# Hybrid decoder layer: the last squares and the token scale of h from GpSimd to VectorE, with the scale's product with ones placed behind a fixed block of matmuls

## Chip, cores and metric

The kernel runs on one core of a Trainium2 chip. The metric is the device time of one execution in microseconds (us). TensorE is called PE, VectorE DVE, ScalarE ACT, GpSimd POOL and SyncE SP, as in the profile.

## What is computed

One layer over 16 meta tokens and 512 tokens of width 2048, in fp32, batch 1. The part that matters here is the seam between the output projection and the feed-forward network:

```python
o = concatenate([_rmsnorm(o_attn, g_attn_out), _rmsnorm(o_conv, g_conv_out)], axis=-1)
h = h + o @ w_out

n2 = _rmsnorm(h, g_ffn)
h = h + (silu(n2 @ w_gate) * (n2 @ w_up)) @ w_down      # D_FF = 5632
```

`_rmsnorm` multiplies a token by `rsqrt(mean(h*h) + 1e-6)` over its 2048 features and by a gain. Before the seam stand an input projection, stick-breaking attention over 8 heads and a gated short convolution.

## The kernel before

Activations are kept transposed: 128 features on the partitions, 512 tokens along the free dimension. Every fp32 operand of a large product is split into a high part (a cast on ACT, line 195 for activations, 652 for weights) and a low part (a subtraction on DVE, lines 196 and 653); a product is three matmuls, high x high, high x low, low x high (lines 750 to 752, and 729 to 731 in the output projection).

**Output projection.** A loop over 16 output tiles of 128 features (`OUT_TILES`). Each tile's two sums are scaled by the scales of the two groups and added to x (`residual`, lines 880 to 884), the result `hj` is written out, its squares are added to `acc_h` (`square_sum`: the square on ACT, line 214, the add on POOL, line 215), and the tile is cut into blocks of 256 tokens, which are mixed (lines 890 to 896, `mixed_blocks`) and split into activations `f0` to `f6`. Two of those seven, `f4` and `f6`, are gathered in DRAM and read back by POOL's DMA queue (`load_f`, line 834). The last tile (`i == KT - 1`) does its residual on DVE at a high priority, then the squares, then the mixed blocks.

**Gate and up.** 44 pairs (`pair_product`), each a Strassen-like product of seven blocks (`block_product`) with 24 matmuls each, on sums of weight quarters. The weight quarters come by SP's DMA queue (line 624); their sums are made on DVE (`add_quads`, line 659; lines 669 and 696), and each load of the next pair goes out when its buffer is free (`load_next`). The first pair takes its blocks in the order of activations 5, 0, 1, 2, 3, 4, 6. DVE combines the blocks out of PSUM between them (lines 781, 785, 788): line 785 reads the bank of `x` between the block on activation 4 and the one on activation 6, which goes on in the same bank.

**The scale of h.** The gain is applied ahead of the products, the token's scale behind them: `r_h`, that is `acc_h` after `h_scale`, multiplies the results of gate and up (lines 959 and 961). `h_scale` is called in the first pair behind the fourth block product (`fourth`). It calls `token_scale`: split `acc_h`, sum it over partitions by two matmuls with ones (lines 511 and 512, tile `ss_h`), add eps on DVE (line 513), then `rsqrt`: Ln and Exp on ACT (lines 202 and 203) and a Newton step of four instructions (lines 204 to 207). For h the low part of the split and the Newton step run on POOL (`eng=gp`), behind the last DMA issue of `load_f(6, 8)` (`tc.issue_after`). The scales of the attention and conv groups run the same function on DVE.

**Order.** A scheduler orders each engine's instructions by priority, data and its own estimates; `tc.high_priority` raises a block's priority, and `tc.keep_in_program_order` fixes an instruction's place on its engine as the program has it. Each engine executes its queue in that order.

## Time and profile before

| | |
|---|---|
| median of 3 runs | 2063.99 us (2063.92 to 2065.08) |
| profiled execution | 2063.16 us, span 2061.5 us |
| granted TensorE clock, mean | 0.999 |
| PE busy | 2048.7 us, 99% of the span |
| DVE busy | 1624.0 us, 79% |
| ACT busy | 1018.5 us, 49% |
| POOL busy | 369.7 us, 18% |

Busy time of PE is the union of pipelined matmuls, so that 99% still holds short waits. A row of the timeline gives start, duration, engine, line, operation, tiles (out<-in) and, in brackets, the idle time of the engine before it and what ended it. Times in the timeline count from the span's start. Buffer numbers are left out of tile names, so `x` is the bank of any pair.

### The profile page before, as it was taken

What the parts mean: (1) busy time and instruction counts of PE and PEld (TensorE: products, weight loads), DVE (VectorE), ACT (ScalarE), POOL (GpSimd) and SP (SyncE); (2) the same over time, 40 slices, a digit from 0 to 9 for tenths busy, and PEclk for the clock granted to TensorE, in tenths of its full rate; (3) what the DMA queues carried; (4) which work ended last, traced back from release to release, by engine and by line L of the source; (5) the groups of instructions that cost most, each with busy time, mean ns of one, the idle gap of its engine ahead of it and who ended that gap; (6) DMA issues with size and microseconds to landing.
All of it is one profiled execution on the core that took longest, in us unless ns stands there. A gap on an engine that the chain in (4) does not pass through costs nothing.

```text
span 2061.5 us, 39375 instructions
## 1 busy us (share of the span) xinstructions
PE 2048.7 (99%) x16086; PEld 1977.6 (96%) x16086; DVE 1624.0 (79%) x2140; ACT 1018.5 (49%) x1529; POOL 369.7 (18%) x490
## 2 busy tenths in 40 slices
PE   9999999999999999999999999999999999999999
PEld 8899999999998888999999999999999999999999
DVE  7877767533336678999898898898888988888888
ACT  7666566322224434555555555555555544444443
POOL 0111111010103445111111011011011243121111
PEclk9999999999999999999999999999999999999999
DMA  5122222222225555546555555465555899798764
GB/s 198 62 82 72 83 72 82 89 93 95 100 104 165 171 166 187 169 135 194 164 146 171 155 164 165 145 181 152 149 175 159 258 333 348 191 302 206 217 149 94
DMA packets 141669, 326.74 MB, mean 159 GB/s; under 512 B 12256, under 2 KB 60128, under 8 KB 141488
## 3 DMA queue, kind: packets, MB, share of 16 engines
q1 hardware_dynamic: 67456, 212.50, 31.9%
q0 software_dynamic: 74032, 111.73, 21.0%
q8 instruction: 126, 2.06, 0.4%
q14 instruction: 55, 0.45, 0.1%
HBM read 258.91 MB, written 65.27 MB: 157 GB/s over the span
## 4 chain that ended last, share of the span: by engine, by line
PE 95%; DVE 2%; DMA 1%; POOL 1%; issue 1%; ACT 1%; DVEq 0%; POOLq 0%; ACTq 0%
PE x L752 11%; PE x L750 11%; PE x L751 11%; PE z L752 5%; PE z L750 5%; PE z L751 5%; PE y L751 3%; PE y L750 3%; PE y L752 3%; PE po L731 3%; PE po L729 3%; PE po L730 3%; PE pv L182 2%; PE pv L184 2%; PE pv L183 2%; PE pu L184 1%
## 5 line engine op out<-in xcount | busy, mean ns | idle before, releaser
L652 ACT CAST sw_split<-sw_in 128x1024 fp32r<-128x1024 f32 (+1 forms) x534 | 527.3, 989 | 535.5 <-PE z L751 164.7
L653 DVE TENSOR_TENSOR sw_split<-sw_in,sw_split 128x1024 fp32r<-128x1024 f32 (+1 forms) x534 | 612.5, 1147 | 98.3 <-ACT sw_split L652 95.3
L752 PE MATMUL x<-f,sw_split 128*128 128x256 f32 x1408 | 388.1, 276 | 2.8 <-DVE sw_split L653 2.8
L750 PE MATMUL x<-f,sw_split 128*128 128x256 f32 x1408 | 388.1, 276 | 0.5 <-DVE u L785 0.3
L751 PE MATMUL x<-f,sw_split 128*128 128x256 f32 x1408 | 387.9, 276 | 0.2 <-DVE f L196 0.2
L752 PEld LDWEIGHTS x<-f,sw_split 128*128 128x128 f32 x1408 | 264.9, 188 | 3.2 <-DVE sw_split L653 3.1
L750 PEld LDWEIGHTS x<-f,sw_split 128*128 128x128 f32 x1408 | 265.0, 188 | 1.0 <-DVE u L785 0.5
L751 PEld LDWEIGHTS x<-f,sw_split 128*128 128x128 f32 x1408 | 264.9, 188 | 0.4 <-DVE f L196 0.4
L149 DVE TENSOR_TENSOR wlo<-raw,whi 128x512 fp32r<-128x512 f32 (+1 forms) x198 | 139.3, 707 | 127.5 <-ACT whi L148 126.9
L950 POOL DMA_DIRECT2D fd<-s x147 | 103.9, 908 | 686.7 <-DVE s L196 685.8
L148 ACT CAST whi<-raw 128x512 fp32r<-128x512 f32 (+1 forms) x198 | 121.4, 615 | 180.1 <-PE pu L183 64.0
L750 PE MATMUL z<-f,sw_split 128*128 128x256 f32 x704 | 193.6, 275 | 0.0
L751 PE MATMUL z<-f,sw_split 128*128 128x256 f32 x704 | 193.6, 275 | 0.0
L752 PE MATMUL z<-f,sw_split 128*128 128x256 f32 x704 | 193.6, 275 | 0.0
L659 DVE TENSOR_TENSOR sw_in<-sw_in 128x1024 f32<-128x1024 f32 (+1 forms) x144 | 164.6, 1143 | 6.9 <-DMA sw_in<-w_down 1.6
L752 PE MATMUL x<-ring,sw_split 128*128 128x256 f32 x608 | 167.3, 275 | 0.5 <-DVE sw_split L653 0.5
L750 PE MATMUL x<-ring,sw_split 128*128 128x256 f32 x608 | 167.2, 275 | 0.0
L751 PE MATMUL x<-ring,sw_split 128*128 128x256 f32 x608 | 167.2, 275 | 0.0
L750 PEld LDWEIGHTS z<-f,sw_split 128*128 128x128 f32 x704 | 132.2, 188 | 0.0
L752 PEld LDWEIGHTS z<-f,sw_split 128*128 128x128 f32 x704 | 132.2, 188 | 0.0
L751 PEld LDWEIGHTS z<-f,sw_split 128*128 128x128 f32 x704 | 132.2, 188 | 0.0
L752 PEld LDWEIGHTS x<-ring,sw_split 128*128 128x128 f32 x608 | 114.1, 188 | 0.7 <-DVE sw_split L653 0.7
(346 smaller groups left out, 5605.8 us busy)
## 6 DMA issues: line engine op xcount, KB each, us to landing
sw_in<-w_gu SPq DMA_DIRECT2D x176, 512.0 KB, 3.8
raw<-w_in SPq DMA_DIRECT2D x92, 512.0 KB, 3.3
fd<-s POOLq DMA_DIRECT2D x147, 256.0 KB, 5.3
sw_in<-w_down SPq DMA_DIRECT2D x96, 384.0 KB, 4.1
ring<-fd POOLq DMA_DIRECT2D x42, 768.0 KB, 16.9
sw_in<-w_out SPq DMA_DIRECT2D x30, 512.0 KB, 3.9
out_T<-d POOLq DMA_DIRECT2D x54, 256.0 KB, 4.6
sw_in<-w_down SPq DMA_DIRECT2D x16, 512.0 KB, 7.9
```

The costliest lines, as they stand in the source:

```text
L148: sc.copy(hi, raw)
L149: ve.tensor_tensor(lo, raw, hi.bitcast(F32), ALU.subtract)
L184: pe.matmul(ps, wl, ah[:, a:b], start=False, stop=k + i == last)
L652: sc.copy(hi, src)
L653: ve.tensor_tensor(lo, src, hi.bitcast(F32), ALU.subtract)
L659: return ve.tensor_tensor(sums[name], a, b, ALU.add)
L729: pe.matmul(ps, hi[:, kk], ah, start=k == 0, stop=False)
L730: pe.matmul(ps, hi[:, kk], al, start=False, stop=False)
L750: pe.matmul(p, hi[:, kk], act[:, 0, k], start=start and j == k == 0, stop=False, skip_group_check=skip)
L751: pe.matmul(p, hi[:, kk], act[:, 1, k], start=False, stop=False, skip_group_check=skip)
L752: pe.matmul(p, lo[:, kk], act[:, 0, k], start=False, stop=k == n - 1, skip_group_check=skip)
L950: gp.dma_start(fd[c][s][:, :, k], t[:, :, i])
```

## The change

The add of the last tile's squares goes to DVE and is written behind the mixed blocks. The token scale of h goes to DVE. Its first matmul with ones is kept in program order, which is behind the first pair's fourth block product. The order behind the last DMA issue of `load_f` is dropped.

```diff
-    def square_sum(acc, src, first, s=None):
+    def square_sum(acc, src, first, s=None, eng=gp):
...
-            gp.tensor_tensor(acc, acc, s, ALU.add)
+            eng.tensor_tensor(acc, acc, s, ALU.add)
...
-    def token_scale(acc, dst, count, name, work, eng=ve):
+    def token_scale(acc, dst, count, name, work, eng=ve, in_order=False):
...
-        pe.matmul(ps, ones_r, sh, start=True, stop=False)
+        first_sum = pe.matmul(ps, ones_r, sh, start=True, stop=False)
+        if in_order:
+            tc.keep_in_program_order(first_sum)
...
             with tc.high_priority(1 << 20):
                 residual(ve)
-                square_sum(acc_h, hj, False, wide_tmp("h", bufs=2))
                 mixed_blocks()
+                square_sum(acc_h, hj, False, wide_tmp("h", bufs=2), ve)
...
-        with tc.high_priority(1 << 20), tc.issue_after(last_f.ins):
-            token_scale(acc_h, acc_h, D, "h", (w[:, 0], w[:, 1], a[:, 0], a[:, 1], b), gp)
+        with tc.high_priority(1 << 20):
+            token_scale(acc_h, acc_h, D, "h", (w[:, 0], w[:, 1], a[:, 0], a[:, 1], b), ve, True)
```

`load_f` no longer returns its last issue. In the built program the same instructions stand on every engine but for six that pass from POOL to DVE. Their order differs only around the seam: on PE the two matmuls with ones stand directly behind the first pair's fourth block product and ahead of the block on activation 4, where before 14 and 16 matmuls of that block stood ahead of them; 13 instead of 5 matmuls of the second pair's first block stand ahead of the first pair's last block. In the next pair the same boundary moves by 6 matmuls. On DVE the order of some 70 instructions changes, and SP's three loads behind the last tile's write go out in another order.

More of the change, by code (lines that the diff above doesn't have):

```diff
@@ L833, in load_f @@
         for part in range(2):
-            last = gp.dma_start(acts[s][:, part, :n], fx[s][:, part, :n], max_dma_last_dim=4096)
-        return last
+            gp.dma_start(acts[s][:, part, :n], fx[s][:, part, :n], max_dma_last_dim=4096)
     after(3, scale_c)
@@ L916, in hybrid_layer @@
                 with tc.high_priority(1 << 20):
-                    last_f = load_f(6, 8)
+                    load_f(6, 8)
         if i < KT - 1:
```

## The prediction

> **What bounds the kernel now.** I read the page first: the share of each engine, then the chain that ended last.

> ```profile
> PE 2048.7 (99%) x16086; PEld 1977.6 (96%) x16086; DVE 1624.0 (79%) x2140; ACT 1018.5 (49%) x1529; POOL 369.7 (18%) x490
> PE 95%; DVE 2%; DMA 1%; POOL 1%; issue 1%; ACT 1%; DVEq 0%; POOLq 0%; ACTq 0%
> ```

> TensorE (PE) sets the time, so a change is worth the TensorE time that it gives back. The view of waits, for PE alone, tells where such time lies.

> ```profile
> PE x L752 <- DVE sw_split L653: 3.3, 3, 2.3
> ...
> PE ss_h L512 <- POOL work_r L196: 1.2, 1, 1.2
> ```

> Both rows belong to the seam between the output projection and the first gate/up pair, where the scale of h is made. The timeline of PE there:

> ```profile
> 797.12 0.28 PE L750 MATMUL z<-f,sw_split 128*128 128x256 f32 x1
> ...
> 799.89 0.28 PE L750 MATMUL x<-f,sw_split 128*128 128x256 f32 x1
> ...
> 802.61 0.28 PE L750 MATMUL z<-f,sw_split 128*128 128x256 f32 x1
> ...
> 805.33 0.28 PE L750 MATMUL x<-f,sw_split 128*128 128x256 f32 x1
> ...
> 807.09 0.50 PE L511 MATMUL ss_h<-work_r,ones_r 128*128 128x512 f32 x1
> 807.42 0.28 PE L752 MATMUL x<-f,sw_split 128*128 128x256 f32 x1
> 807.54 0.28 PE L750 MATMUL x<-f,sw_split 128*128 128x256 f32 x1
> 809.05 0.50 PE L512 MATMUL ss_h<-work_r,ones_r 128*128 128x512 f32 x1 [1.23 <-POOL work_r L196]
> ...
> 812.07 0.38 PE L750 MATMUL x<-f,sw_split 128*128 128x256 f32 x1 [0.32 <-DVE u L785]
> ...
> 819.93 0.28 PE L751 MATMUL x<-f,sw_split 128*128 128x256 f32 x1
> 822.54 0.58 PE L752 MATMUL x<-f,sw_split 128*128 128x256 f32 x1 [2.34 <-DVE sw_split L653]
> ...
> 825.48 0.33 PE L750 MATMUL x<-f,sw_split 128*128 128x256 f32 x1
> ...
> 826.60 0.28 PE L750 MATMUL z<-f,sw_split 128*128 128x256 f32 x1
> ```

> A block of 24 products takes 2.72 us undisturbed (799.89 to 802.61), a product 0.113. From 797.12 to 826.60, 29.48 us, PE did eight blocks (8 x 2.72 = 21.8) and the two products with ones (0.23 each by their spacing): 22.2 us of work, so **7.3 us were lost**. That is the most that the change can bring, but for the wait of the first products on the last tile (near 796), which it leaves alone. Of it 2.5 us is the hole from 820.0 to 822.54, and 1.4 the slow products behind it: 13 steps from 822.54 to 825.48 took 2.94 us, where 13 x 0.113 = 1.5 would do. The view by windows shows that clock:

> ```profile
> 822.50:825.60 3.10, 3.06 (x14) 3.06 (x15) 3.10 (x4) 2.42 (x3) 0.00 (x0) 0.50 0.11 18
> ```

> (columns: window, length, busy PE, PEld, DVE, ACT, POOL, granted clock, DMA share, GB/s.) The clock was halved after the hole.

> **What is removed.** GpSimd's timeline has the six moved instructions (L215, L196, L204 to L207); three of them, and the L215 of the tile before:

> ```profile
> 786.17 1.28 POOL L215 TENSOR_TENSOR acc_h<-acc_h,sw_in 128x512 f32<-128x512 f32 x1 [0.46 <-ACT sw_in L214]
> ...
> 796.03 9.21 POOL L215 TENSOR_TENSOR acc_h<-acc_h,w 128x512 f32<-128x512 f32 x1 [2.41 <-ACT w L214]
> 807.11 1.89 POOL L196 TENSOR_TENSOR work_r<-acc_h,work_r 128x512 fp32r<-128x512 f32 x1 [1.87 <-ACT work_r L195]
> ...
> 815.53 2.16 POOL L205 TENSOR_TENSOR work_b<-work_b,work_a 128x512 f32<-128x512 f32 x1
> ```

> The add of the last squares took 9.21 us against 1.28 one tile earlier, while VectorE was full. It delays the two products; PE then waits 1.23 for the low part, and the hole at 820 comes from the last four instructions, which VectorE waits for with its weight splits queued behind (row 820.66 below). All of that goes. GpSimd has only DMA issues left, and these wait for VectorE's data; the order behind the reload's last issue, which the edit also drops, had no other use.

> **What is added.** VectorE (DVE), timeline:

> ```profile
> 792.17 0.68 DVE L881 TENSOR_TENSOR w<-w,sw_in 128x512 f32<-128x512 f32 x1
> 792.76 1.22 DVE L653 TENSOR_TENSOR sw_split<-sw_in,sw_split 128x1024 fp32r<-128x1024 f32 x1
> 793.90 0.69 DVE L883 TENSOR_TENSOR w<-w,sw_in 128x512 f32<-128x512 f32 x1
> ...
> 796.31 0.42 DVE L196 TENSOR_TENSOR f<-src,f 128x256 fp32r<-128x256 f32 x1
> 796.64 1.22 DVE L659 TENSOR_TENSOR sw_in<-sw_in 128x1024 f32<-128x1024 f32 x1
> ...
> 805.52 1.23 DVE L659 TENSOR_TENSOR sw_in<-sw_in 128x1024 f32<-128x1024 f32 x1 [1.43 <-DMA sw_in<-w_gu]
> ...
> 807.79 1.49 DVE L196 TENSOR_TENSOR f<-src,f 128x256 fp32r<-128x256 f32 x1
> ...
> 816.45 2.32 DVE L659 TENSOR_TENSOR sw_in<-sw_in 128x1024 f32<-128x1024 f32 x1
> 820.66 0.69 DVE L959 TENSOR_TENSOR u<-u,acc_h 128x512 f32<-128x512 f32 x1 [1.89 <-POOL acc_h L207]
> ```

> In a full queue a 128x512 instruction takes 0.60 us of VectorE (792.17 to 792.76), a 128x1024 one 1.135 (792.76 to 793.90), a 128x256 one 0.335 (796.31 to 796.64). Five of the six cost 0.60; L206 ran on VectorE in the scale of the conv group:

> ```profile
> L206 DVE TENSOR_SCALAR sw_in<-sw_in x1: 427/427/427, 633.2 to 633.2; 128x512 f32<-128x512 f32 x1
> ```

> so 0.34 of queue. Together 3.3 us. Against that, VectorE's own instructions beside GpSimd's were stretched: 807.79 by 1.07 (1.49 against 0.42) and 816.45 by 1.10. Those 2.2 us come back.

> **Walk through the new order.** In the built program the new VectorE order from 796.64 on is: L215, L653, L196, L669, L893, L653, L196, L895, L659, L196, L196, L788, L653, L196 (the low part of acc_h), L653, L781, L513, L653, L659, L204, L785. The squares are there (ScalarE's L214 had released GpSimd at 796.0). The first twelve are four of 128x1024 (4.54), seven of 128x256 (2.35) and L215 (0.60): 796.64 + 7.5 = 804.1. The split L653 of the sixth weight needs its cast by ScalarE, which can start when L659 ends (803.2):

> ```profile
> 802.75 1.06 ACT L652 CAST sw_split<-sw_in 128x1024 fp32r<-128x1024 f32 x1 [0.55 <-PE x L751]
> ```

> so cast to 804.3, L653 from 804.35 to 805.5, and the low part of acc_h ends at 805.5 + 0.68 = 806.2. The two products with ones now stand ahead of the whole block that starts at 805.33. The first goes at once, as its cast of acc_h is done by 804.9; the second, due at 805.56, waits to 806.2, and every product of the first two pairs is queued behind it, where before 14 products of the next block ran ahead of the first and 16 ahead of the second: **0.65 lost**, and 0.1 at the first product after a wait (807.42 came 0.33 behind 807.09, not 0.23). Then L653 (806.1), L781 (807.2), L513 (807.55; its sums are there from 806.7, so it holds nothing up), L653 (808.15), L659 (809.3), L204 (810.4; Ln and Exp end near 809.6), L785 from 811.0 to 811.45. PE meanwhile runs the block to 806.45 + 2.72 = 809.2, then 13 products of the next pair's first block, which the program puts there, to 810.65; the seventh block of the pair needs L785: **0.8 + 0.1 lost**. The next pair's L785 stands behind L205 to L207 and the gate work that this delays; nothing in before shows its wait. Bounds: 0, and another 0.9; I take 0.45, halfway, as VectorE has no idle time left up to there in the walk. The 0.1 at the first product with ones included, the new order loses 0.75 + 0.9 + 0.45 + 0.1 = 2.2 us. **The sum: 7.3 - 2.2 = 5.1 us less.** L204 to L207 now end near 816, and the first scaling L959 waits for nothing; no hole near 820, so no halved clock.

> **The load that moves.** The add L659 of the first pair's third mixed weight goes behind L669, so the three weight loads that their buffers release go out in another order: the one that the next pair's L659 (809.3 in the walk) reads is last of three, not first, and issued at 803.6 instead of 797.89.

> ```profile
> 797.89 0.33 SPq L624 DMA_DIRECT2D sw_in<-w_gu  x1
> sw_in<-w_gu SPq DMA_DIRECT2D x176, 512.0 KB, 3.8
> f<-fx POOLq DMA_DIRECT2D x2, 1024.0 KB, 12.6
> GB/s 289 283 238 156 88 263 378 401 416 430 401 401 437 394 361 370 418 397 401 393 438 393 418 385 385 393 410 418 426 410 410 410 410 418 221 33 25 0 0 0
> ```

> (the last row: 790 to 810 us in 40 slices.) It took 7.6 us in before (797.89 to 805.5), under the reload of the activations; the median of all is 3.8. So it lands between 807.4 and 811.2, and costs 0 to 1.9 us. I take 0: the transfers run at some 400 GB/s to 807.3 and then stop, and the bytes are the same, so the last load lands near 808, over 1 us early.

> The profiled execution took 2063.16, 1.66 over its span, and becomes 2058.1; the median of the runs shown is 0.83 higher: **2058.9 us**. 0.2% is 4.1 us, about what a measurement of this kernel can tell from no change.

> **The rivals.** *Late load.* The moved load takes 7.6 us again: VectorE stops at L659, L785 follows, PE loses 1.9 more: 2060.8. For it speaks the same reload; against it, that the reload is nearly through by 803.6.

> *No halved clock in the timed runs.* A hole of 2.5 us halved the clock here, for about 3 us. If the hole lies otherwise to whatever measures it, before does not pay the 1.4, and the gain is 3.7: 2060.3. [...]

> *VectorE becomes the bound (slower).* In the pairs that follow VectorE is nearly full:

> ```profile
> 830.00:840.00 10.00, 10.00 (x91) 10.00 (x90) 9.07 (x12) 4.51 (x6) 0.00 (x0) 1.00 0.68 203
> 840.00:850.00 10.00, 10.00 (x91) 10.00 (x90) 9.90 (x12) 6.30 (x9) 0.95 (x2) 1.00 0.16 55
> ```

> If its backlog is not worked off, each of the 42 pairs behind the second loses 0.45 at its L785 too: 18.9 - 5.1 = 13.8 us more, 2077.8; slower than before from twelve such pairs on (5.1 / 0.45). Against it: a pair takes PE seven blocks, 19.0 us, and the busy shares of 91% and 99% overstate VectorE, since the 12 instructions of a row overlap by 0.09 each (85% without that); some 2.9 us a pair are free, so the backlog goes in a pair or two.

> *No effect.* PE's lost time returns at other waits, as L785 moved: within 1 us of 2064.

> **How the numbers follow.** Forecast 0.72 (nine tenths of it beyond 4.1 us), late load 0.08, no halved clock 0.12, no effect 0.04, VectorE the bound 0.04. Faster by over 0.2%: 0.65; within: 0.31; slower: 0.04. The range: at the low end only the wait for the low part of acc_h stays, 7.3 - 0.85 = 6.4 us less, 2057.6; at the high end late load and no halved clock together, 5.1 - 1.9 - 1.4 = 1.8 less, 2062.2.

> **What would show it.** Right: L215 on VectorE near 796.6 in some 0.68; L512 waiting about 0.65 for DVE, no longer POOL; a wait at L750 for L785 of 0.7 to 0.9; no wait over 2 us and no clock of 0.5 near 822; the 826.60 row some 5 us earlier. Wrong: a wait of L659 for its load near 810, a new hole over 1 us, waits for L785 in pair after pair, or the end unmoved though the seam is shorter.

## The result, and the profile after

| | before | after |
|---|---|---|
| median of the timed runs | 2064.74 us (8 runs, 2063.92 to 2065.85) | 2058.67 us (8 runs, 2058.21 to 2059.78) |
| profiled execution | 2063.16 us, span 2061.5 | 2058.70 us, span 2056.9 |

The ratio is 0.9972, with a 95% interval of 0.9963 to 0.9981: 5.8 us faster by the ratio, 6.1 by the medians, against 5.1 forecast from the seam. The two profiled executions differ by 4.5 us.

In the kernel after, line numbers behind 511 are two higher than before (512 is 514, 653 is 655, 659 is 661, 750 to 752 are 752 to 754, 785 is 787), and one higher behind `load_f` (959 is 960). So the rows named L752 here are the high x high products that were L750. The page's shares and the chain of the kernel after:

```profile
PE 2046.7 (100%) x16086; PEld 1976.0 (96%) x16086; DVE 1623.2 (79%) x2146; ACT 1016.0 (49%) x1529; POOL 351.5 (17%) x484
PE 96%; DVE 2%; ACT 1%; issue 1%; DMA 0%; POOL 0%; SPq 0%; DVEq 0%; ACTq 0%; POOLq 0%
```

GpSimd (POOL) has six instructions fewer and VectorE (DVE) six more; GpSimd, with 1% of the chain before, has 0% now. The view of waits for PE, cut to the seam:

```profile
PE x L752 <- DVE u L787: 1.5, 2, 1.3
PE ss_h L514 <- DVE work_r L196: 0.5, 1, 0.5
```

The 2.3 us wait for VectorE's weight split and the 1.2 us wait for GpSimd's subtraction are gone; three shorter ones, of 1.32, 0.49 and 0.21 us, stand in their place (the first row holds two). The timeline of PE there, with the products in front of each wait (start, duration):

```profile
805.22 0.40 PE L511 MATMUL ss_h<-work_r,ones_r 128*128 128x512 f32 x1
806.11 0.50 PE L514 MATMUL ss_h<-work_r,ones_r 128*128 128x512 f32 x1 [0.49 <-DVE work_r L196]
806.45 0.28 PE L752 MATMUL x<-f,sw_split 128*128 128x256 f32 x1
...
810.56 0.28 PE L752 MATMUL x<-f,sw_split 128*128 128x256 f32 x1
812.15 0.39 PE L752 MATMUL x<-f,sw_split 128*128 128x256 f32 x1 [1.32 <-DVE u L787]
...
830.43 0.28 PE L754 MATMUL x<-f,sw_split 128*128 128x256 f32 x1
830.91 0.38 PE L752 MATMUL x<-f,sw_split 128*128 128x256 f32 x1 [0.21 <-DVE u L787]
```

By spacing, with 0.23 us for a product with ones and 0.113 for another, the first wait costs 0.89 - 0.23 = 0.66 us, the product behind it 0.11 more, the second wait 1.59 - 0.11 = 1.48 and the third 0.48 - 0.11 = 0.37. The clock stays whole where it was halved before (windows, column PEclk):

```profile
822.50:825.60 3.10, 3.10 (x30) 3.10 (x29) 2.56 (x3) 1.65 (x3) 0.00 (x0) 1.00 0.09 12
```

VectorE's timeline shows why the second wait is longer than the forecast's 0.8:

```profile
796.54 0.68 DVE L215 TENSOR_TENSOR acc_h<-acc_h,w 128x512 f32<-128x512 f32 x1
...
805.37 0.68 DVE L196 TENSOR_TENSOR work_r<-acc_h,work_r 128x512 fp32r<-128x512 f32 x1
...
809.94 1.22 DVE L661 TENSOR_TENSOR sw_in<-sw_in 128x1024 f32<-128x1024 f32 x1 [0.69 <-DMA sw_in<-w_gu]
811.08 0.68 DVE L204 TENSOR_TENSOR work_b<-work_a 128x512 f32<-128x512 f32 x1
811.68 0.42 DVE L787 SCALAR_TENSOR_TENSOR u<-x,sides 128x256 f32<-128x256 f32 x1
...
821.50 0.68 DVE L960 TENSOR_TENSOR u<-u,acc_h 128x512 f32<-128x512 f32 x1
```

Up to the low part of `acc_h` (805.37) all is as walked. Then L661 waits 0.69 us for its weights, the load that the change moved, and L787, which PE waits for, is as much later. The first scaling, L960, waits for nothing any more.

To compare executions, take the starts of matmuls number 5000 and 5500 (counted from 0, in order of start), on either side of the seam; before, then after:

```profile
791.16 0.28 PE L751 MATMUL y<-f,sw_split 128*128 128x256 f32 x1
856.29 0.28 PE L751 MATMUL x<-f,sw_split 128*128 128x256 f32 x1
```

```profile
791.05 0.28 PE L753 MATMUL y<-f,sw_split 128*128 128x256 f32 x1
851.92 0.28 PE L753 MATMUL x<-f,sw_split 128*128 128x256 f32 x1
```

That is 65.1 us of seam before and 60.9 after. The stretch from matmul 5500 to the last took 1201.0 and 1200.9. All profiled executions of this study can be cut so (us; the last column is the whole profiled execution):

| kernel (label of its run) | start of no. 100 | 100 to 5000 | seam, 5000 to 5500 | 5500 to last | time |
|---|---|---|---|---|---|
| before | 20.20 | 770.95 | 65.14 | 1201.02 | 2063.16 |
| before_again | 20.12 | 771.05 | 66.03 | 1200.87 | 2063.93 |
| before_third | 21.19 | 771.04 | 64.78 | 1201.04 | 2063.90 |
| before_fourth | 20.91 | 771.05 | 65.13 | 1200.87 | 2063.81 |
| after | 20.08 | 770.97 | 60.87 | 1200.86 | 2058.70 |
| after_again | 20.10 | 771.02 | 60.40 | 1201.07 | 2058.74 |
| squares_only | 20.79 | 770.93 | 64.68 | 1200.87 | 2063.11 |
| scale_only | 20.16 | 771.05 | 62.26 | 1200.89 | 2060.62 |
| scale_only_again | 21.00 | 771.09 | 62.27 | 1201.16 | 2061.78 |
| newton_gp | 20.13 | 771.04 | 63.58 | 1201.23 | 2062.20 |
| newton_gp_again | 20.25 | 771.00 | 63.27 | 1201.02 | 2061.79 |
| free_sum | 19.66 | 771.05 | 60.83 | 1200.86 | 2058.32 |
| t3_before | 20.16 | 770.94 | 65.30 | 1200.86 | 2063.10 |
| l785_high | 20.21 | 771.02 | 60.25 | 1200.31 | 2057.84 |

Two columns vary: the seam, which the change is about, and the first 20 us, the program's first loads and products, which no kernel here touches and which ended anywhere from 19.66 to 21.19 us. The seam went from 65.3 (mean of four) to 60.6 (mean of two): **4.6 us** is what the profiles show of the change.

### The profile page after: what moved, and what is told of

The parts are those of the page before. It is cut to its first block, busy times and chain, and to the rows that moved or that the text cites. A ratio compares the mean times of both kernels' runs of the same rounds, so it can differ in the third digit from the quotient of the medians.

```text
span 2056.9 us, 39370 instructions
## 1 busy us (share of the span) xinstructions
PE 2046.7 (100%) x16086; PEld 1976.0 (96%) x16086; DVE 1623.2 (79%) x2146; ACT 1016.0 (49%) x1529; POOL 351.5 (17%) x484
## 3 DMA queue, kind: packets, MB, share of 16 engines
HBM read 258.91 MB, written 65.27 MB: 158 GB/s over the span
## 4 chain that ended last, share of the span: by engine, by line
PE 96%; DVE 2%; ACT 1%; issue 1%; DMA 0%; POOL 0%; SPq 0%; DVEq 0%; ACTq 0%; POOLq 0%
PE x L752 11%; PE x L754 11%; PE x L753 11%; PE z L752 6%; PE z L753 6%; PE z L754 6%; PE y L752 3%; PE y L753 3%; PE y L754 3%; PE po L732 3%; PE po L733 3%; PE po L731 3%; PE pv L182 2%; PE pv L184 2%; PE pv L183 2%; PE pu L184 1%
## 5 line engine op out<-in xcount | busy, mean ns | idle before, releaser
L752 PE MATMUL x<-f,sw_split 128*128 128x256 f32 x1408 | 387.6, 275 | 1.8 <-DVE u L787 1.5
L752 PEld LDWEIGHTS x<-f,sw_split 128*128 128x128 f32 x1408 | 264.3, 188 | 2.3 <-DVE u L787 1.9
L752 PE MATMUL z<-f,sw_split 128*128 128x256 f32 x704 | 193.6, 275 | 0.0
L661 DVE TENSOR_TENSOR sw_in<-sw_in 128x1024 f32<-128x1024 f32 (+1 forms) x144 | 163.4, 1134 | 5.5 <-DMA sw_in<-w_down 0.8
L752 PE MATMUL x<-ring,sw_split 128*128 128x256 f32 x608 | 167.2, 275 | 0.0
L752 PEld LDWEIGHTS z<-f,sw_split 128*128 128x128 f32 x704 | 132.2, 188 | 0.0
## 6 DMA issues: line engine op xcount, KB each, us to landing
sw_in<-w_gu SPq DMA_DIRECT2D x176, 512.0 KB, 3.7
raw<-w_in SPq DMA_DIRECT2D x92, 512.0 KB, 3.3
sw_in<-w_out SPq DMA_DIRECT2D x30, 512.0 KB, 4.0
sw_in<-w_down SPq DMA_DIRECT2D x16, 512.0 KB, 7.8
```

The costliest lines, as they stand in the source:

```text
L661: return ve.tensor_tensor(sums[name], a, b, ALU.add)
L752: pe.matmul(p, hi[:, kk], act[:, 0, k], start=start and j == k == 0, stop=False, skip_group_check=skip)
```

## The experiments

**The theory after the result:** the seam's losses came from GpSimd's part of the scale, above all from the Newton step; VectorE does the same six instructions in 3.3 us and gives back most of the time. Rivals: the 9.21 us add of the squares was the loss, or the scale's new place on PE was the gain, or the half clock was.

### The kernel before, again: before_again, before_third, before_fourth

No edit.

> The kernel before, unchanged, to see how its hole near 820 us and the halved clock behind it vary between executions. Theory (the halved clock depends on how the hole lies to a measuring stretch): the hole is again 2.3 to 2.6 us, but the granted clock behind it, or elsewhere near the seam, differs from the first profile, and the executions that are slower than the first profiled one (2063.16 us) lose the difference there; between 0 and 3 us at half clock. Rival (the spread of the runs lies elsewhere): the seam from 797 to 827 us takes 29.5 us again with the same 1.4 us at half clock, and a time above 2064 shows outside the seam.

It took 2063.93 us. The hole is there again, the half clock is not, and the add took another course. GpSimd, VectorE and PE near 796:

```profile
796.04 1.50 POOL L215 TENSOR_TENSOR acc_h<-acc_h,w 128x512 f32<-128x512 f32 x1 [2.41 <-ACT w L214]
808.19 1.82 POOL L196 TENSOR_TENSOR work_r<-acc_h,work_r 128x512 fp32r<-128x512 f32 x1 [10.66 <-ACT work_r L195]
```

```profile
796.33 1.49 DVE L196 TENSOR_TENSOR f<-src,f 128x256 fp32r<-128x256 f32 x1
```

```profile
797.87 0.39 PE L751 MATMUL x<-f,sw_split 128*128 128x256 f32 x1 [1.26 <-DVE f L196]
```

The add took 1.50 us instead of 9.21, VectorE's L196 beside it 1.49 instead of 0.42, and PE stood 1.07 us longer for it (1.64 between the two products' starts, 0.57 otherwise). So there are two outcomes, called the race for the add from here on: 9.21 us on GpSimd with 0.42 on VectorE, or 1.50 with 1.49. And with the add done at 797.5, GpSimd idled 10.66 us and began its subtraction no sooner: **the add by itself delayed nothing**, because ACT's cast of `acc_h` (L195, at 807.50 here) stands later in its queue.

> The kernel before, unedited, profiled a third time: its timed runs lie from 2062.4 to 2065.4 us, and two profiled executions showed different losses (2063.16 with 3.4 us at half clock behind the 2.6 us hole and GpSimd's add at 9.21 us; 2063.93 with no half clock, the add at 1.50 and PE standing 1.07 longer at 797). Theory: the add's outcome (0 or 1.1 us) and the half clock (0, or 1.4 to 1.7 for a stretch of 3.4 us, twice that for 6.8) vary from execution to execution, and the time follows: a third profile shows one of the four combinations, with the hole of 2.6 us in it every time; 2062 to 2066. Rival: the losses go with the program, and the profile repeats one of the two shown with a time that they don't explain.

> The kernel before, unedited, profiled a fourth time, as in the third: the hole of 2.6 us at the same product; the add at either about 9.2 or about 1.5 us, and in the second case 1.07 us more at the product at 797; a stretch at half clock or none; time 2062 to 2066, the higher the more of the two it has.

They took 2063.90 and 2063.81 us, with the add at 9.21 us in both, and the hole of 2.61 us between starts. The third had no half clock, the fourth had it; the windows behind the hole, third and then fourth:

```profile
823.50:826.70 3.20, 2.64 (x22) 2.45 (x22) 3.20 (x4) 2.71 (x3) 0.00 (x0) 1.00 0.22 42
```

```profile
823.50:826.70 3.20, 3.20 (x16) 3.20 (x16) 3.17 (x5) 2.95 (x4) 0.00 (x0) 0.50 0.23 51
```

PE was busy for all 3.20 us at half clock (16 products), and for 2.64 at full clock (22). What filled the rest is in PE's and ACT's timeline of the third:

```profile
827.16 0.39 PE L750 MATMUL z<-f,sw_split 128*128 128x256 f32 x1 [1.01 <-ACT sides L777]
```

```profile
823.97 1.28 ACT L962 ACT_TABLE_LOAD   x1 [4.33 <-DVE g L961]
825.27 0.64 ACT L962 ACTIVATE g<-g 128x512 f32<-128x512 f32 x1
825.81 1.03 ACT L652 CAST sw_split<-sw_in 128x1024 fp32r<-128x1024 f32 x1
826.74 0.36 ACT L777 COPY sides<-z 128x256 f32<-128x256 f32 x1
```

At full clock PE reaches the block on `z` earlier and there waits 1.01 us for ACT's copy, which stands behind the gate's table load and activation, which waited 4.33 us for VectorE's L961, which follows the Newton step. In PE's timeline the hundredth product behind the hole started 12.90 and 13.12 us after it in the two executions with half clock, 12.81 in both without: the half clock cost 0.1 to 0.3 us, not 1.4. Both losses have one cause, the late scale.

The mean granted clock on record for each timed run says the same: a stretch of 3.4 us at half clock lowers the mean over 2061 us to 0.999. Of the 49 runs of before in the two larger sets, 17 had 1.0 and took 2063.8 us in the mean; 32 had 0.999 or 0.998 and took 2064.2. All 16 timed runs of the kernel after had 1.0.

Of the theory on the spread, the parts varied as expected, but not the time with them: what moved it were the add's race (66.03 of seam against 65.0) and the first 20 us (up to 1.1).

### The squares alone on VectorE: squares_only

The edit is against the kernel before.

```diff
-                square_sum(acc_h, hj, False, wide_tmp("h", bufs=2))
                 mixed_blocks()
+                square_sum(acc_h, hj, False, wide_tmp("h", bufs=2), ve)
```

> The change's first part alone: the last tile's add of squares on VectorE behind the mixed blocks; the split's low part and the Newton step of the scale of h stay on GpSimd, the product with ones free. Theory (the time was lost to what GpSimd does behind the add: the low part and the Newton step, with VectorE's weight splits queued behind the first scaling): PE waits for the low part from GpSimd for over 1 us and again 2 to 3 us at a hole while the Newton step runs on GpSimd, so hardly anything is gained: 2063 to 2066 us. Rival (the 9.21 us add of squares was the whole cost, since all else waits for it): most of the gain is there, 2058.5 to 2060.

2063.02 us, a ratio of 0.9994 (0.9986 to 1.0003): no gain that can be measured. PE's timeline:

```profile
805.43 0.50 PE L511 MATMUL ss_h<-work_r,ones_r 128*128 128x512 f32 x1 [1.07 <-ACT work_r L195]
807.29 0.80 PE L514 MATMUL ss_h<-work_r,ones_r 128*128 128x512 f32 x1 [1.13 <-POOL work_r L196]
814.63 0.39 PE L754 MATMUL x<-f,sw_split 128*128 128x256 f32 x1 [1.05 <-DVE sw_split L655]
823.85 0.38 PE L752 MATMUL x<-f,sw_split 128*128 128x256 f32 x1 [0.96 <-ACT sides L777]
```

The first product with ones comes 1.7 us earlier, and the waits are split up but remain: GpSimd's subtraction, its Newton step behind VectorE's weight split, ACT's copy. The rival that the add was the loss falls. The clock was halved here too, from 806.8 to 810.2, and the seam of 64.68 has that in it.

### The scale alone on VectorE: scale_only, scale_only_again

The edit is against the kernel before.

```diff
-        with tc.high_priority(1 << 20), tc.issue_after(last_f.ins):
-            token_scale(acc_h, acc_h, D, "h", (w[:, 0], w[:, 1], a[:, 0], a[:, 1], b), gp)
+        with tc.high_priority(1 << 20):
+            token_scale(acc_h, acc_h, D, "h", (w[:, 0], w[:, 1], a[:, 0], a[:, 1], b), ve, True)
```

> The change's second part alone: split, Newton step and the placed product on VectorE as in the changed kernel; the last tile's add of squares stays on GpSimd ahead of the mixed blocks. Theory (the hole came from the Newton step on GpSimd, and the add of squares is late but can be borne): the add still takes some 9 us, the product's low part is waited for by 1 to 1.5 us, but no hole over 2 us and no halved clock: 2058 to 2060 us. Rival (the 9.21 us add was the whole cost): 2063 to 2065. Second rival (both parts are needed, each gives about half): 2061 to 2062.

2061.04 us, 0.9987 (0.9978 to 0.9996). The hole is gone; 3.0 us of the seam's 4.6 are there without the squares. What is missing is in PE's waits:

```profile
797.92 0.38 PE L753 MATMUL x<-f,sw_split 128*128 128x256 f32 x1 [1.26 <-DVE f L196]
811.76 0.50 PE L514 MATMUL ss_h<-work_r,ones_r 128*128 128x512 f32 x1 [2.01 <-DVE work_r L196]
```

The first is the race for the add again (1.50 us on GpSimd here). The second is the low part of `acc_h`: it is at 811.02 on VectorE, behind three more weight instructions and a wait of 1.40 us for a load, where the whole change has it at 805.37. So the squares on VectorE are worth 1.6 us with the scale there, most of it the race, and 0.6 without it (65.27 against 64.68).

> The scale alone on VectorE, with the square add left on GpSimd, profiled again. The first profile took 2060.6 us with the add at 1.50 us, 1.07 us more at 797 and a wait of 2.0 us at the second product with ones; its runs lie from 2059.3 to 2063.7. Theory: with the add at 9.2 us the stall at 797 is gone and the time is 2059.3 to 2059.6, unless the clock is halved behind the 2.0 us wait, which adds 1.7 or more. Rival: the add's outcome doesn't move the end and the time is 2060.6 with either.

2061.78 us, with the add at 1.50 us again, so the outcome at 9.2 was not seen and the question of its price in this kernel stays open. The clock was halved here, from about 800.2 to 803.6, yet the seam is the same to 0.01 us (62.27 against 62.26): the products came later to the second product with ones, and its wait shrank from 2.01 us to 0.3. The 1.16 us between the two executions lie at the start (0.84) and behind the seam (0.27).

### The Newton step back on GpSimd: newton_gp, newton_gp_again

The edit is against the kernel after; the scale of h passes `gp` as `late`.

```diff
-    def token_scale(acc, dst, count, name, work, eng=ve, in_order=False):
+    def token_scale(acc, dst, count, name, work, eng=ve, in_order=False, late=None):
...
-        rsqrt(dst, v, SEQ, y, t, eng)
+        rsqrt(dst, v, SEQ, y, t, late or eng)
```

> The changed kernel with only the four instructions of the Newton step put back on GpSimd; squares, low part and the placed product stay as changed. Theory (the Newton step on GpSimd makes the hole): the wait for the low part stays at 0.5 us, but acc_h is ready only after 5 to 7 us on GpSimd, VectorE waits at the first scaling with weight splits behind it, PE has a hole of 2 to 3.5 us and, if that halves the clock, 1.4 more: 2062 to 2065. Rival (the late start of the scale, not its pace, made the hole): the scale starts 5 us earlier here, so there is no hole: 2058.5 to 2060.

2063.64 us, 0.9998 (0.9989 to 1.0007): with four of the six instructions back on GpSimd the whole gain is gone in the timed runs, and 2.8 of 4.6 us in the seam. PE and VectorE:

```profile
806.23 0.50 PE L514 MATMUL ss_h<-work_r,ones_r 128*128 128x512 f32 x1 [0.49 <-DVE work_r L196]
812.17 0.38 PE L752 MATMUL x<-f,sw_split 128*128 128x256 f32 x1 [1.76 <-DVE u L787]
822.20 0.39 PE L752 MATMUL x<-f,sw_split 128*128 128x256 f32 x1 [2.48 <-ACT sides L777]
```

```profile
816.08 0.69 DVE L960 TENSOR_TENSOR u<-u,acc_h 128x512 f32<-128x512 f32 x1 [1.90 <-POOL acc_h L207]
```

The hole is back at the same place in the chain: L207 on GpSimd, L960 on VectorE, the gate on ACT, and PE last. Here it ends at ACT's copy, before it ended at VectorE's split behind L959; both are queued behind the scale.

> The change with the Newton step's four instructions on GpSimd, profiled again. Its first profile took 2062.2 us and showed no half clock, but the median of its runs was 2063.6. Theory: behind its 2.0 and 2.75 us waits the clock is halved in some executions, so that this profile shows a stretch at half clock of 3.4 us (2063.6 to 2064) or none (2062.2). Rival: the median is higher for a reason that the profile would show elsewhere, with no half clock at 2063.6 or more.

2061.79 us: again no half clock, though the hole's wait was now 3.42 us long. Yet the timed runs tie the median, 1.4 to 1.9 us above both profiled executions, to the half clock. Of the 11 timed runs of newton_gp, three had a mean granted clock of 1.0 and took 2062.20 to 2062.44 us; the other eight had 0.999 or 0.998 and took 2063.02 to 2064.91. Both profiled executions are of the first kind.

### Repeated, and three variants: after_again, free_sum, t3_before, l785_high

The first is the kernel after, unedited; the edits of the other three are against it.

> The changed kernel once more, unedited, beside the other kernels of this set, so that they can be set against it on the same chip in the same session. 2058.7 us, a ratio of 0.997 to the kernel before. Its profile should again show no hole of over 1 us on PE after the fifth product's wait, no stretch at half clock, and the square add on VectorE at 0.68 us. If one of the 9.21/1.50 us outcomes that the kernel before shows on GpSimd or a half-clock stretch is found here too, the change did not remove them.

2058.59 us, 0.9973 (0.9963 to 0.9984), and the profile as expected. Its one difference from the first:

```profile
809.52 1.23 DVE L661 TENSOR_TENSOR sw_in<-sw_in 128x1024 f32<-128x1024 f32 x1 [0.20 <-DMA sw_in<-w_gu]
```

```profile
811.74 0.39 PE L752 MATMUL x<-f,sw_split 128*128 128x256 f32 x1 [0.84 <-DVE u L787]
```

The moved load came 0.49 us sooner, and PE's wait is 0.48 shorter, 0.84: the late load goes one to one into it.

**The product with ones left to the scheduler** (free_sum):

```diff
-            token_scale(acc_h, acc_h, D, "h", (w[:, 0], w[:, 1], a[:, 0], a[:, 1], b), ve, True)
+            token_scale(acc_h, acc_h, D, "h", (w[:, 0], w[:, 1], a[:, 0], a[:, 1], b), ve)
```

> The change without its placed product: the scale's first product with ones is left to the scheduler, which puts it ahead of the pair's fourth product, where its operand is not yet there. Theory: the place is worth nothing by itself as long as the whole scale is on VectorE; the wait moves from the second product (0.66 us) to the first (about 1.4), the wait of the pair's next products for VectorE's combine falls from 1.5 to 0.5, and the rest of the scale runs earlier. Sum of the waits 2.7 against 2.5 us: 2058.5 to 2059.2, the same as the changed kernel. Rival: the place is what the gain needs, as PE stands behind the early product: 2060.5 or more (at least the 1.4 us on top and the following product's wait unshortened).

2058.95 us, 0.9975 (0.9965 to 0.9985), a seam of 60.83. PE now waits 1.08 us at the first product with ones and 0.26 at the pair's last block:

```profile
804.42 0.50 PE L511 MATMUL ss_h<-work_r,ones_r 128*128 128x512 f32 x1 [1.08 <-ACT work_r L195]
812.04 0.38 PE L752 MATMUL x<-f,sw_split 128*128 128x256 f32 x1 [0.26 <-DVE u L787]
```

The place on PE is worth nothing that can be told: the wait is moved, not removed. The rival falls.

**VectorE's sums in the order of before** (t3_before), so that the moved load goes out first again:

```diff
-        t3 = add_quads(i, "t3", b["12"], b["22"])
+        t3 = kept["t3"] = add_quads(i, "t3", b["12"], b["22"])
...
-        ve.tensor_tensor(sums["t2"], sums["t2"], b["21"], ALU.add)
+        with tc.issue_after(kept["t3"].ins):
+            ve.tensor_tensor(sums["t2"], sums["t2"], b["21"], ALU.add)
```

> The change with VectorE's sum of two weight blocks put back ahead of the next one, as the kernel before had it, so that the load that follows it is issued before the other again and should be in memory when VectorE reaches the next sum (0.69 us of VectorE's idle time before the 1.22 us sum at 809.94 in the changed kernel). Theory: the order of the loads costs the changed kernel at most the 0.7 us; but with this order VectorE reaches the low part of the accumulator some 4 us later (810 rather than 805.4), and PE's second product with ones waits about 2 us for it instead of 0.66: 2059.5 to 2060.2, some 0.9 us slower than the changed kernel. Rival: the late load is the larger loss and its removal outweighs: 2058.0 or less.

2062.09 us, 0.9989 (0.9980 to 0.9997): most of the gain is lost, 2 us more than expected. PE's longest wait is 1.78 us for the low part of `acc_h`. The load is there sooner, at 806.99 instead of 809.94, but VectorE comes to its sum sooner still, waits 2.36 us, and all that is queued behind it is late (rows of PE, VectorE and the windows):

```profile
812.13 0.79 PE L514 MATMUL ss_h<-work_r,ones_r 128*128 128x512 f32 x1 [1.78 <-DVE work_r L196]
```

```profile
806.99 1.23 DVE L661 TENSOR_TENSOR sw_in<-sw_in 128x1024 f32<-128x1024 f32 x1 [2.36 <-DMA sw_in<-w_gu]
```

```profile
811.50:818.30 6.80, 6.17 (x28) 6.07 (x29) 6.22 (x8) 1.26 (x2) 0.00 (x0) 0.50 0.25 80
```

The missing 2 us are the half clock, from 811.5 to 818.3, which no later wait hides here. From the second product with ones to the hundredth behind it PE took 14.49 us, against 11.74 in scale_only at whole clock: 2.75 us. Without them the profiled 2063.10 would be about 2060.35, an estimate just over the expected 2059.5 to 2060.2. The timed runs bear it out: three of 11 had a mean granted clock of 1.0 and took 2060.00 to 2061.15 us, the other eight had less and took 2061.72 to 2063.10.

There is more in this run. It moves no work between engines, yet without its half clock its seam is still 62.55 us (65.30 - 2.75), some 1.9 longer than the change's 60.6. So with the scale on VectorE about 2 of the 4.6 us still hang on VectorE's order, which the scheduler changed along with the edit and which puts the low part of `acc_h` at 805.37 instead of 811.40.

**The combine ahead of the Newton step** (l785_high):

```diff
-        ve.scalar_tensor_tensor(c2[:, 1], x, -1.0, p5, ALU.mult, ALU.subtract)
+        with tc.high_priority(1 << 21):
+            ve.scalar_tensor_tensor(c2[:, 1], x, -1.0, p5, ALU.mult, ALU.subtract)
```

> The changed kernel with VectorE's combine of the sixth side (the sum from the fifth product) at the higher priority, so that it stands ahead of the Newton step's first instruction in the first pair, and ahead of the other queued work in the next pair. Theory: the change's remaining losses are this combine's place in VectorE's queue: 0.6 of the 1.48 us wait at 812.15 and most of the 0.37 us one at 830.91 come back, 0.6 to 1.0 us: 2057.7 to 2058.1. Rival: the wait was set by something else (the late load, or ACT's copies) and the time stays at 2058.7; a second rival is that the later pairs, where the same combine now goes first too, lose what is won here: 2058.7 or slower.

2058.17 us (2057.84 to 2058.56, 6 runs), 0.9970 (0.9959 to 0.9982): the lowest median, 0.4 us under the changed kernel beside it, with runs that overlap (2058.32 to 2059.45 there). In the first pair the combine is at 810.61 and PE waits 0.60, not 0.84 or 1.32:

```profile
811.08 0.39 PE L752 MATMUL x<-f,sw_split 128*128 128x256 f32 x1 [0.60 <-DVE u L788]
```

The seam won only 0.15 us over the better execution of the change, as the next pair's wait stayed. The rest lies near 1707 us, where the changed kernel has

```profile
1707.34 0.36 PE L752 MATMUL x<-first,sw_split 128*128 128x256 f32 x1 [0.28 <-DVE d_first L787]
```

and l785_high no wait: the same combine, in a later pair. Half of the theory held.

## Why the prediction was right

The forecast was 2058.9 us and the median 2058.67. Two things that it had named as signs of being wrong did appear, in small: L661 waiting for its load near 810, and one new wait of over 1 us on PE. By its steps:

- **PE's lost 7.3 us at the seam, and what goes.** Right in size. The hole was the Newton step's, as said: newton_gp brings it back (2.48 and 3.42 us of wait). "It delays the two products", said of the add, was wrong: with an add of 1.50 us they came no earlier. With the add on VectorE the first of them came 1.7 us earlier, and still nothing was gained that can be measured. Its real price is the race: 1.07 us at 797 in one of four executions of before, and in both of scale_only.
- **The half clock, 1.4 us.** Right as a part of this execution's sum, wrong as a part that could be missing alone. Without it PE waits 1.01 us for ACT, and the seam is as long (64.8 to 65.1 with the slow add in all three). So the rival *no halved clock in the timed runs* fell: before does run without it in 17 of 49 runs, which are only 0.4 us faster than the others and still some 5 us slower than the kernel after, not 3.7. In newton_gp the two groups of runs lie 1.6 us apart in the mean.
- **VectorE's cost.** Right: instructions of 0.68 us and the low part of `acc_h` ending at 806.05, against 806.2.
- **The new waits.** L514: 0.65 + 0.1 forecast, 0.66 + 0.11 measured. The next pair's combine: 0.45 taken, a halfway guess that came near by luck, 0.37 measured. The first pair's: 0.8 + 0.1 forecast, 1.48 measured by spacing, 1.00 in after_again.
- **The load that moves: the mis-sized term.** I took 0, because the transfers "stop" near 807.3 and the last load would land near 808. Bulk did stop there; the load's end did not. The row of before in the prediction has such a tail too, 33 and 25 GB/s up to 808.5. The windows of the changed kernel:

```profile
807.00:808.00 1.00, 1.00 (x11) 1.00 (x10) 1.00 (x3) 0.00 (x0) 0.00 (x0) 1.00 0.69 283
808.00:809.00 1.00, 1.00 (x12) 1.00 (x11) 1.00 (x2) 0.81 (x2) 0.00 (x0) 1.00 0.07 29
809.00:810.00 1.00, 1.00 (x12) 1.00 (x11) 0.32 (x2) 0.46 (x1) 0.00 (x0) 1.00 0.02 8
```

A DMA share of 0.07 of 16 engines is one engine. The trace has the packets: from 808.2 to 809.45 they run one at a time, and VectorE waited to 809.94 (0.69 us; 0.20 in after_again). The load, issued at 803.55, took some 6.4 us. The rival *late load* named this mechanism and priced it at 1.9; it cost 0.69, about a third of that.
- **The sum.** New losses 2.2 forecast; 0.66 + 0.11 + 1.48 + 0.37 = 2.6 measured, 2.15 in after_again. The gain by the seam is 4.6, a little under 5.1.
- **The median.** The medians moved by 6.1 us, and by 5.9 in the set of after_again, more than the seam. Two of four profiled executions of before began 0.7 to 1.1 us late and one lost 1.07 to the race; neither execution of after did. With the add on VectorE (0.68 us in after) PE's product near 797 waits 0.18 us for L196 there, not 1.26, and the race is gone; whether the late start is chance is not settled. That the forecast hit the median to 0.2 us is partly luck: the seam gave less and the rest more than it said.
- **VectorE becomes the bound; no effect.** Both fell: the waits for the combine end with the second pair, but for one of 0.28 us at 1707. The 2.9 us a pair that the argument gave VectorE were too many. Two windows of 19 us in before (859 to 878 and 878 to 897) have it busy for 16.98 and 18.22 us, which leaves 2.0 and 0.8; it was enough.

## What to carry to other kernels

Price a small serial step on a slow engine by the queue behind its result, not by its busy time: four GpSimd instructions of 1.29 to 2.16 us each (0.42 to 0.68 on VectorE in after) held VectorE's splits, ACT's gate and in the end PE. When an edit lets the scheduler reorder a queue, test the order by itself: here it held about 2 of the 4.6 us. Before counting a loss as removable by itself (a half clock, a late product), look for the next wait on the same path, follow it in a second profile of the same kernel, and sort the timed runs by their granted clock. A fall of the bandwidth did not mean that the load had landed: in after the bulk was through near 808, the load's packets ran one at a time to 809.45, and VectorE waited to 809.94. Read the DMA share's tail.

## What the runs showed of the hardware

**Two engines, two outcomes.** The same add on GpSimd took 9.21 us in three profiled executions of before, and 1.50 in the fourth and in both of scale_only. VectorE's 128x256 subtraction beside it took 0.42 us in before, where the add took 9.21, and 1.49 and 1.50 in before_again and scale_only, where it took 1.50. At 9.21 us the add ended only when VectorE paused for a load: in before it ran from 796.03 to 805.24, and VectorE, behind eleven instructions from 796.31 on without a pause, was idle from 804.09 to 805.52; in before_third it ran from 797.10 to 806.31, and VectorE was idle for the 1.17 us up to 806.32. What decides between the outcomes was not shown.
